# A third, half-width set of k-tiles in the seven-product input projection of an attention layer

## The chip, the cores and the metric

One core of a Trainium2 chip runs one program. The metric is device microseconds (us) of that program, the median of several runs, beside one execution taken by the hardware profiler. Engines: TensorE (PE, with its weight loads PEld), VectorE (DVE), ScalarE (ACT), GpSimd (POOL), SyncE (SP) and 16 DMA engines.

## The reference

Two layers on 256 tokens of width 2048, in fp32: a Mamba2 mixer, then a forgetting-attention mixer, each added to the input, and a last norm. The attention is what the change touches:

```python
h = rmsnorm(x, w)                                  # 256 x 2048
proj = h @ w_in                                    # 2048 x (4 * 4096 + 32): q, k, v, z, forget
log_f = log_sigmoid(f_logit + b_forget); cum = cumsum(log_f)
logits = q @ k.T * scale + cum[query] - cum[key]   # 32 heads of 128, causal
o = softmax(logits) @ v * silu(z)
x = x + o @ w_out
```

## The kernel before

Each fp32 product is made of three in a faster format: a weight tile `raw` is split into a high part `wh` (ACT, `act_hi`, L104) and a low part `wl` (DVE, `dve_lo`, L110), activations likewise, and TensorE adds high x high, high x low and low x high in one PSUM bank (`product`, L130). A weight tile is 128 x 1024: two k-tiles (128 rows of the weight) by 512 columns. Every tile is loaded once, by SP's queue, into one of seven buffers called `raw`; there are five `wh` and four `wl` buffers.

The attention's input projection is done in 16 blocks: for each of eight groups of four heads, a block of q and k and a block of v and z (`block_units`). A block has two token tiles of 128 and two column halves, L and R, of 512. The first `KS` = 8 of the 16 k-tiles are done by seven products of sums in place of eight (a fast matrix product over pairs of k-tiles by pairs of token tiles by column halves): two sets of four k-tiles each. A step such as `A1` makes one of the seven weight sums and multiplies it by one of seven activation sums, the "forms", which are built once (`x2_tiles`, `form_x`, `split_form`) and held in the pool `forms` of six buffers. Weight sums are three chains: "a" is loaded (A0), a term is added by an accumulating DMA of POOL's queue (A1), the sum "b" by DVE (A3, L181), another term by POOL (A2); "b" is loaded (B0) and added to (B1); "c" is loaded (C0). The other eight k-tiles are done plainly, in parts of 12 matmuls, "L" and "R", of two k-tiles each. A step on one set has six matmuls.

`STEPS` writes out the order of a block's steps by hand; `FIRST` is that of the first block, which also holds the forget gate's product and the switch to the attention's pool of buffers. `run` splits the tile of the part three ahead (`AHEAD`) before a part's matmuls, so that ACT and DVE run ahead of TensorE as far as `wh`, `wl` and `raw` buffers are free. Other work is hung on these parts by due times (`later`, `emit_due`, counted in half parts); the instructions of an engine run in program order.

Between the blocks lies the attention of four heads (`four_heads`). For each pair of heads, `load_cum` fetches the cumulated forget logs, broadcast to all partitions (`cB`); `logits` adds them, the query's own sums `cum_q` and the causal mask in two DVE instructions per head (L1142) to a tile `dd`, which `softmax` adds to the scores. After groups 1 to 5 comes one output stage of eight parts (`out_f`), and three follow at the end. So a steady cycle is one q/k block, one v/z block and one output stage.

Of the kernel before, what the change touches and what calls it, by code (L numbers as in the profile page):

```python
# [11 lines left out]
F32 = mybir.dt.float32  # L12
# [5 lines left out]
P = 128  # L18
# [16 lines left out]
C_S = {64: C_MN + 384, 32: C_MN + 384 + 64}  # L35
# [10 lines left out]
KS = 8  # L46
# [3 lines left out]
def constants():  # L50
    c = np.zeros((P, C_N), np.float32)
    i = np.arange(P)
    j, t = i[:, None], i[None, :]
    c[:, C_ID:C_ID + P] = np.eye(P)
    c[:, C_CC:C_CC + P] = ((j >= 64) & (j <= t)) * 1.0 - ((j < 64) & (j > t)) * 1.0
    c[:, C_U:C_U + P] = j > t
    tri = (j <= t) * 1.0
    c[:, C_MQ:C_MQ + 384] = np.concatenate([tri, np.ones((P, P)), tri], 1) * 0.25
    low = np.where(t <= j, 0.0, NEG)
    c[:, C_MN:C_MN + 384] = np.concatenate([low, np.zeros((P, P)), low], 1)  # L60
# [7 lines left out]
def hybrid_kernel(ctx: ExitStack, tc: tile.TileContext, a):  # L68
# [69 lines left out]
    def prep(u, h, pieces=1, first=False):  # L138

        raw = wp.tile([P, 1024], F32, tag="raw", name="raw", bufs=RAW)
        wh = wp.tile([P, 1024], F32R, tag="wh", name="wh")
        m, n = u.get("both", (1024, 0))
        wl = wp.tile([P, 1024], F32R, tag="wl", name="wl", bufs=4) if 2 * n < m else None
        wide = 1024 // m * (m - n)
        for i in range(pieces):
            c = slice(i * wide // pieces, (i + 1) * wide // pieces)
            k = slice(i * 1024 // m // pieces, (i + 1) * 1024 // m // pieces)
            nc.sync.dma_start(raw[:, c], u["src"][:, h * wide + c.start:h * wide + c.stop])  # L150
            if not n:
                act_hi(wh[:, c], raw[:, c])
                dve_lo(wl[:, c], raw[:, c], wh[:, c])
                continue
            r = raw[:, c].rearrange("p (k m) -> p k m", m=m - n)
            hi = wh.rearrange("p (k m) -> p k m", m=m)[:, k]
            if first and i == 0:
                nc.vector.tensor_copy(hi[:, :, :m - n], r)
            else:
                act_hi(hi[:, :, :m - n], r)  # L160
            dve_lo(hi[:, :, m - n:], r[:, :, m - 2 * n:], hi[:, :, m - 2 * n:m - n])
            if wl is not None:
                lo = wl.rearrange("p (k m) -> p k m", m=m)[:, k]
                dve_lo(lo[:, :, :m - 2 * n], r[:, :, :m - 2 * n], hi[:, :, :m - 2 * n])
            if i + 1 < pieces:
                yield
        u["w"][h] = (wh, wl)

    def prep_sum(u):


        name, src, how = u["chain"]
        if how == "load":
            u["sums"][name] = (
                fp[0].tile([P, 1024], F32, tag="sum", name=f"sum_{name}") if u.get("apart") else
                wp.tile([P, 1024], F32, tag="raw", name=f"sum_{name}", bufs=RAW))
            nc.sync.dma_start(u["sums"][name], src)
        elif how == "add":
            behind["POOL"] = nc.gpsimd.dma_start(u["sums"][name], src, accum_op=ALU.add).ins  # L179
# [3 lines left out]
        wh = wp.tile([P, 1024], F32R, tag="wh", name="wh")  # L183
        wl = wp.tile([P, 1024], F32R, tag="wl", name="wl", bufs=4)
        act_hi(wh, raw)
        behind["DVE"] = dve_lo(wl, raw, wh).ins
        u["w"][0] = (wh, wl)
        yield
# [74 lines left out]
    def split_form(f, summed, held, g, name):  # L263
# [8 lines left out]
        gh, gl = (gp.tile([P, 7, P], F32R, tag=f"g{i}", name=f"g{i}{name}") for i in "hl")  # L272
# [30 lines left out]
    def joined(out, ps, scale):  # L303

        n = out.shape[0]
        rest = sp.tile([P, S], F32, tag="rest", name="rest")[:n, :]
# [39 lines left out]
    def ktile(x, k):  # L346

        return x[k // 4][:, k % 4]
# [4 lines left out]
    def row_scale(rst, name, pool=cp):  # L353
# [51 lines left out]
    def xt_split(tag):  # L405
        return [bp.tile([P, 4, 2, S], F32R, tag=f"x{q}", name=f"x{tag}_{q}") for q in range(4)]
# [474 lines left out]
    def x2_tiles(k0):  # L881
# [29 lines left out]
    def stats2():  # L911
# [10 lines left out]
        lay2["rstB"] = row_scale(r, "rstB2")  # L922


    cum_q = cp.tile([P, T2, FH], F32, name="cum_q")
# [18 lines left out]
    def forget_sums(lf):  # L944
# [7 lines left out]
        pq = bank(psa, "pq")  # L952
        nc.tensor.matmul(pq[:, 0:FH], tri, lf[:, 0, :], start=True, stop=True)
# [20 lines left out]
    STEPS = (A0, C0, "L", B0, "L", "L", A1, "L", A3, "R", "R", "R", B1, A2, "R")  # L974
    FIRST = (0, "L", "L", 1, "L", A0, C0, B0, "L", "enter", A1, A3, "R", "R", "R", B1, A2, "R")

    def block_units(w_s, w_p, out, scale, done, order):
# [3 lines left out]
        ps, held, sums = {}, {}, ({}, {})  # L981
        us = {c: [{"src": w_p[i][m], "w": [None, None]} for m in range((KT - KS) // 4)]
              for i, c in enumerate("LR")}

# [19 lines left out]
        def mm_sum(u, form, name, p2):  # L1004
            wh, wl = u["w"][0]
            first = start(name)
            for i, w in enumerate((wh, wh, wl)):
                for p in range(2):
                    y = lay2["forms"][0][2 * p2 + p][i % 2]
                    product(ps[name], y[:, form, :], w[:, p * 512:p * 512 + 512],  # L1010
                            start=first and i == p == 0, stop=p2 == p == 1 and i == 2,
                            skip_group_check=True)

        def mm_rest(u, n, names):
            wh, wl = u["w"][n % 2]
            first = [start(name) for name in names]
            for i, w in enumerate((wh, wh, wl)):
                for k2 in range(2):
                    k = KS + 2 * n + k2
                    for t, name in enumerate(names):  # L1020
# [3 lines left out]
                                stop=2 * n + k2 == KT - KS - 1 and i == 2 and name != "y",  # L1024
# [17 lines left out]
        for step in order[0]:  # L1042
# [6 lines left out]
            if step in n_rest:  # L1049
# [10 lines left out]
            for p2 in range(2):  # L1060
                u = {"chain": (chain, w_s[p2, term], how), "sums": sums[p2], "w": [None],
                     "apart": chain == "b" and p2 == 0 and order[0] is STEPS}
                parts.append({"u": u, "h": [0], "long": 1,
                              "mm": lambda u=u, form=form, name=name, p2=p2:
                                  mm_sum(u, form, name, p2)})
            if (chain, term) in reads:
                parts[-1]["post"] = reads[chain, term]
        if "enter" in order[0]:
# [3 lines left out]
    def four_heads(hq, first=()):  # L1072
# [7 lines left out]
        def vz_done(c):  # L1080
# [3 lines left out]
            vh = fp[0].tile([P, 512], F32R, tag="vh", name=f"vh{hq}")  # L1084
            vl = fp[0].tile([P, 512], F32R, tag="vl", name=f"vl{hq}")
# [19 lines left out]
        def load_cum(i2):  # L1105
            cb = fp[0].tile([P, 2, S], F32, tag="cB", name=f"cB{hq}_{i2}", bufs=2)
            h = 4 * hq + 2 * i2
            with tc.issue_after(behind["POOL"]):
                nc.gpsimd.dma_start(cb, cum_d[h:h + 2, :].partition_broadcast(P))
            st[f"c{i2}"] = cb  # L1110
# [19 lines left out]
        def logits(i):  # L1130
# [5 lines left out]
            h = 4 * hq + i  # L1136
            st["dd"] = dd = fp[0].tile([P, 384], F32, tag="dd", name="dd")
            cb = st[f"c{i // 2}"][:, i % 2, :]
            mk = cst[:, C_MN:C_MN + 384]
            with tc.issue_after(st["split"]):  # L1140
                for t, c, n in BLOCKS:
                    nc.vector.scalar_tensor_tensor(  # L1142
                        dd[:, c:c + n], cb[:, :n], cum_q[:, t, h:h + 1], mk[:, c:c + n],
                        op0=ALU.add, op1=ALU.add)
# [54 lines left out]
        def close(i):  # L1199
# [15 lines left out]
        return [block_units(a["wf_s"][hq, n], a["wf_p"][hq, n], out, scale, done,  # L1215
# [90 lines left out]
def packed(x, norm_w, m_w_in, m_conv_w, m_conv_b, m_dt_bias, m_A_log, m_D,  # L1306
# [46 lines left out]
    def by_k(w):  # L1355
# [13 lines left out]
        "wf_s": np.stack([qk[0], vz[0]], 1), "wf_p": np.stack([qk[1], vz[1]], 1),  # L1369
# [19 lines left out]
```

## Time and profile before

| what | before |
|---|---|
| median of 3 runs | 1591.97 us (1591.59 to 1593.38) |
| the profiled execution's own time | 1592.1 us |
| its span, first to last instruction | 1590.3 us |
| granted TensorE clock | 0.999 |
| HBM read | 357.29 MB, 226 GB/s over the span |
| instructions | 22604 |

How to read it: the span is the time from the first to the last instruction. Busy time is a sum over one engine's instructions; matmuls are pipelined and their ends are modelled, so a TensorE that is always busy need not be at its peak. The chain of waits is followed back from the last instruction to what released it. Rows of transfers give their size and the median time from issue to landing. In a timeline an idle time in brackets stands with what ended it.

### The profile page before, as it was taken

How to read it: one execution, taken by the hardware profiler on the slowest of the kernel's cores; microseconds unless marked ns; L12 is line 12 of the kernel's file. 1: busy time of each engine (PE TensorE's matmuls, PEld its weight loads, DVE VectorE, ACT ScalarE, POOL GpSimd, SP SyncE). 2: the span in 40 equal slices, each digit the busy share in tenths (PEclk: the TensorE clock that was granted, in tenths of full speed). 3: DMA queues.
4: the chain of work that ended last, by engine and by line, in shares of the span. 5: the costliest groups of instructions: out<-in, count | busy, mean ns of one | idle time of the engine just before them, and what ended most of it. 6: DMA issues, size and time to landing. Idle time of an engine off the chain costs nothing.

```text
span 1590.3 us, 22604 instructions
## 1 busy us (share of the span) xinstructions
PE 1576.8 (99%) x7808; PEld 1326.1 (83%) x7808; DVE 1332.9 (84%) x2016; ACT 1058.3 (67%) x1624; POOL 164.7 (10%) x211
## 2 busy tenths in 40 slices
PE   9999999999999999999999999999999999999997
PEld 7888888888888888878888888888888888888886
DVE  6898989798989898788887887878878887888886
ACT  7677676767676765766776675666666666666764
POOL 0000111011100110011110110110110111011100
PEclk9999999999999999999999999999999999999999
DMA  9665798769886987579887887797886887898842
GB/s 369 193 214 189 192 270 221 265 175 273 222 262 182 269 216 236 187 172 251 265 235 252 223 213 247 223 247 213 222 261 187 251 253 182 237 263 242 260 164 80
DMA packets 100356, 360.98 MB, mean 227 GB/s; under 512 B 11505, under 2 KB 12401, under 8 KB 100113
## 3 DMA queue, kind: packets, MB, share of 16 engines
q1 hardware_dynamic: 75312, 270.16, 48.4%
q0 software_dynamic: 24784, 89.24, 29.6%
q8 instruction: 61, 1.00, 0.2%
q14 instruction: 55, 0.44, 0.1%
q10 hardware_dynamic: 144, 0.13, 0.0%
HBM read 357.29 MB, written 2.20 MB: 226 GB/s over the span
## 4 chain that ended last, share of the span: by engine, by line
PE 97%; DVE 1%; issue 0%; DMA 0%; ACT 0%; SPq 0%; ACTq 0%; POOLq 0%; POOL 0%
PE psa L130 24%; PE pst L130 17%; PE psx L130 12%; PE psz L130 10%; PE psv L130 9%; PE psu L130 8%; PE psy L130 8%; PE py L682 2%; PE pqk L1117 1%; PE psc L1135 1%; PE ppt L1171 1%; PE po L1197 0%; PE pof L687 0%; PE psc L1133 0%; PE pyt L737 0%; PE pxa L632 0%
## 5 line engine op out<-in xcount | busy, mean ns | idle before, releaser
L104 ACT ACTIVATE wh<-raw 128x1024 fp32r<-128x1024 f32 (+2 forms) x371 | 390.3, 1054 | 210.1 <-PE psa L130 62.5
L110 DVE TENSOR_TENSOR wl<-raw,wh 128x1024 fp32r<-128x1024 f32 (+2 forms) x371 | 447.2, 1211 | 61.5 <-issue 29.2
L104 ACT ACTIVATE wh<-sum_a 128x1024 fp32r<-128x1024 f32 x176 | 185.4, 1056 | 130.6 <-PE psy L130 29.2
L110 DVE TENSOR_TENSOR wl<-sum_a,wh 128x1024 fp32r<-128x1024 f32 x176 | 214.7, 1222 | 61.2 <-PE psu L130 40.4
L130 PE MATMUL pst<-x,wh 128*128 128x512 f32 (+1 forms) x800 | 203.2, 394 | 2.1 <-ACT wh L104 1.3
L130 PEld LDWEIGHTS pst<-x,wh 128*128 128x128 f32 (+1 forms) x800 | 144.6, 187 | 31.9 <-ACT wh L104 1.9
L130 PE MATMUL psa<-wh,x 128*128 128x512 f32 x512 | 129.5, 392 | 0.0
L104 ACT ACTIVATE wh<-sum_b 128x1024 fp32r<-128x1024 f32 x88 | 93.3, 1060 | 51.9 <-PE psx L130 29.9
L110 DVE TENSOR_TENSOR wl<-sum_b,wh 128x1024 fp32r<-128x1024 f32 x88 | 106.5, 1219 | 10.5 <-issue 9.4
L130 PEld LDWEIGHTS pst<-x,wl 128*128 128x128 f32 x768 | 105.8, 190 | 9.0 <-DVE wl L110 0.9
L130 PEld LDWEIGHTS psa<-wh,x 128*128 128x128 f32 x512 | 95.3, 188 | 20.5 <-DVE cu L308 0.6
L130 PE MATMUL pst<-x,wl 128*128 128x256 f32 x768 | 109.1, 282 | 0.0
L179 POOL DMA_DIRECT2D sum_a<-in_wf_s x64 | 56.1, 878 | 470.0 <-DVE wl L110 311.7
L130 PE MATMUL psz<-wh,x 128*128 128x512 f32 x256 | 100.4, 392 | 0.0
L130 PE MATMUL psv<-wh,x 128*128 128x512 f32 x256 | 99.8, 390 | 0.0
L130 PE MATMUL psu<-wh,x 128*128 128x512 f32 x256 | 99.8, 390 | 0.0
L130 PE MATMUL psy<-wh,x 128*128 128x512 f32 x256 | 99.7, 389 | 0.0
L775 DVE TENSOR_TENSOR xs<-psa,xs 128x512 f32<-128x512 f32 (+1 forms) x81 | 52.0, 679 | 31.7 <-PE psa L130 31.6
L130 PE MATMUL psa<-wh,ghf 128*128 128x512 f32 (+1 forms) x260 | 71.0, 392 | 0.0
L130 PE MATMUL psa<-wl,x 128*128 128x512 f32 x256 | 69.3, 391 | 1.1 <-DVE wl L110 1.0
L130 PE MATMUL psa<-wh,glf 128*128 128x512 f32 (+1 forms) x260 | 69.6, 386 | 0.0
L130 PE MATMUL psa<-wl,ghf 128*128 128x512 f32 (+1 forms) x260 | 69.6, 386 | 0.0
(360 smaller groups left out, 3250.4 us busy)
## 6 DMA issues: line engine op xcount, KB each, us to landing
raw<-in_wf_p SPq DMA_DIRECT2D x128, 512.0 KB, 5.0
raw<-in_wm_t SPq DMA_DIRECT2D x90, 512.0 KB, 5.4
raw<-in_wm_z SPq DMA_DIRECT2D x64, 512.0 KB, 5.7
sum_a<-in_wf_s POOLq DMA_DIRECT2D x64, 512.0 KB, 8.3
raw<-in_wf_o SPq DMA_DIRECT2D x64, 512.0 KB, 5.5
sum_a<-in_wm_s POOLq DMA_DIRECT2D x36, 512.0 KB, 7.4
sum_a<-in_wf_s SPq DMA_DIRECT2D x32, 512.0 KB, 7.6
sum_c<-in_wf_s SPq DMA_DIRECT2D x32, 512.0 KB, 5.9
```

Source lines behind the costliest of these rows:

```text
L104: nc.scalar.activation(out, in_, AF.Copy)
L110: return nc.vector.tensor_tensor(out, in_, hi.bitcast(F32), op=ALU.subtract)
L130: behind["PE"] = nc.tensor.matmul(*args, **kw).ins
L179: behind["POOL"] = nc.gpsimd.dma_start(u["sums"][name], src, accum_op=ALU.add).ins
L682: nc.tensor.matmul(st["py"][t][:, c], m[:, j, t, :], st["xd"][:, t, c], start=True, stop=True)
L775: nc.vector.tensor_tensor(c, pss[t][:, a:b], c, op=ALU.add)
L1117: nc.tensor.transpose(pt[:, n * P:n * P + P], st["qk"][:, t, c:c + FD], ident)
L1135: nc.tensor.matmul(ps[:, P:P + S], q[:, :P], k[:, P:], start=j == 0, stop=j == 2)
L1171: nc.tensor.transpose(pt[:, c:c + P], uu[:, c:c + P], ident)
```

## The change

- `KS` becomes 10 in all blocks but the first: k-tiles 8 and 9 form a third set, half as wide (one pair of k-tiles, weight tiles of 128 x 512). Its steps have three matmuls. The first block keeps 8 k-tiles, with its own weights `wf_b`. L and R have three parts each in place of four, and the order of the steps is new: A2 is last.
- The third set's sums lie in the sixth buffer of the pool `forms` ("a" with tag `gh`, "b" with tag `gl`); its "c" takes a `raw` buffer. A fifth form is built; its unsplit values take a `raw` buffer for that time.
- The query's own sums are left out (`cum_q` and its three products): they are the same for a whole row of the softmax. The cumulated logs are loaded straight into `dd`, now two buffers for two heads each, and the mask is added to two heads by one DVE instruction.
- Buffers move to make room: the activations' k-tiles are cut 4, 4, 2, 2, 4, and `vh`, `vl` take the place of k-tiles 8 and 9; `rest`, `cu`, `vt` and the row of scales move to the Mamba pool; split outputs of groups 0 to 5 move from `forms` to the attention's pool.

```diff
-KS = 8
+KS = 10
+KS0 = 8
+X_AT = (0, 4, 8, 10, 12)
...
         name, src, how = u["chain"]
+        wide = u.get("wide", 1024)
         if how == "load":
-            u["sums"][name] = (
-                fp[0].tile([P, 1024], F32, tag="sum", name=f"sum_{name}") if u.get("apart") else
-                wp.tile([P, 1024], F32, tag="raw", name=f"sum_{name}", bufs=RAW))
+            if u.get("apart"):
+                t = fp[0].tile([P, 1024], F32, tag="sum", name=f"sum_{name}")
+            elif wide < 1024 and name != "c":
+                t = gp.tile([P, 7, P], F32, tag="gh" if name == "a" else "gl",
+                            name=f"sum_{name}").rearrange("p m s -> p (m s)")
+            else:
+                t = wp.tile([P, 1024], F32, tag="raw", name=f"sum_{name}", bufs=RAW)
+            u["sums"][name] = t[:, :wide]
...
-        gh, gl = (gp.tile([P, 7, P], F32R, tag=f"g{i}", name=f"g{i}{name}") for i in "hl")
+        if pool is None:
+            gh, gl = (gp.tile([P, 7, P], F32R, tag=f"g{i}", name=f"g{i}{name}") for i in "hl")
+        else:
+            gh, gl = (pool.tile([P, 4, P], F32R, tag=f"f{i}", name=f"g{i}{name}", bufs=2)
+                      for i in "hl")
...
-            f = lp.tile([P, 4 * (S + 1)], F32, tag=("xa", "xa", "xd", "zs")[k0 // 2],
-                        name="form", bufs=2 if k0 < 4 else 1)
+            f = (lp.tile([P, 4 * (S + 1)], F32, tag=("xa", "xa", "xd", "zs")[k0 // 2],
+                         name="form", bufs=2 if k0 < 4 else 1) if k0 < 8 else
+                 wp.tile([P, 1024], F32, tag="raw", name="form", bufs=RAW))
...
-        pq = bank(psa, "pq")
-        nc.tensor.matmul(pq[:, 0:FH], tri, lf[:, 0, :], start=True, stop=True)
-        nc.tensor.matmul(pq[:, FH:2 * FH], ones, lf[:, 0, :], start=True, stop=False)
-        nc.tensor.matmul(pq[:, FH:2 * FH], tri, lf[:, 1, :], start=False, stop=True)
-        nc.scalar.copy(cum_q.rearrange("p t h -> p (t h)"), pq[:, :2 * FH])
...
-    STEPS = (A0, C0, "L", B0, "L", "L", A1, "L", A3, "R", "R", "R", B1, A2, "R")
+    STEPS = (A0, C0, "L", B0, "L", A1, "L", A3, "R", "R", B1, "R", A2)
...
         def right():
             add("z", 0, 1, ALU.subtract)
             add("u", 1, 1, ALU.subtract, 0)
+
+        def last():
             add("y", 1, 0)
             done(held["out"])
...
-            for p2 in range(2):
-                u = {"chain": (chain, w_s[p2, term], how), "sums": sums[p2], "w": [None],
+            for p2 in range(len(pairs)):
+                u = {"chain": (chain, w_s[p2][term], how), "sums": sums[p2], "w": [None],
+                     "wide": 512 * pairs[p2],
                      "apart": chain == "b" and p2 == 0 and order[0] is STEPS}
-                parts.append({"u": u, "h": [0], "long": 1,
+                steps[0] += pairs[p2] == 1
+                parts.append({"u": u, "h": [0], "long": 1 if pairs[p2] == 2 else steps[0] % 2,
...
-            with tc.issue_after(st["split"]):
-                for t, c, n in BLOCKS:
-                    nc.vector.scalar_tensor_tensor(
-                        dd[:, c:c + n], cb[:, :n], cum_q[:, t, h:h + 1], mk[:, c:c + n],
-                        op0=ALU.add, op1=ALU.add)
+            if i % 2 == 0:
+                dd = st[f"d{i // 2}"].rearrange("p h (b s) -> p h b s", b=3)
+                mk = cst[:, C_MN:C_MN + P].unsqueeze(1).unsqueeze(1).to_broadcast([P, 2, 2, P])
+                with tc.issue_after(st["split"]):
+                    nc.vector.tensor_tensor(dd[:, :, 0:3:2], dd[:, :, 1:3], mk, op=ALU.add)
...
+        def weights(n):
+            s1, s2 = a["wf_s"][hq, n], a["wf_h"][hq, n]
+            half = lambda c, m: a["wf_p"][hq, n, c][:, m * 1024:m * 1024 + 1024]
+            rest = [[half(c, m) for m in range((KT - KS) // 2)] for c in range(2)]
+            if hq == n == 0:
+                return [s1[0], s1[1]], [[a["wf_b"][c], *rest[c]] for c in range(2)]
+            return [s1[0], s1[1], s2], rest
```

More of the change, by code (lines that the diff above doesn't have):

```diff
@@ L59, in constants @@
     low = np.where(t <= j, 0.0, NEG)
-    c[:, C_MN:C_MN + 384] = np.concatenate([low, np.zeros((P, P)), low], 1)
+    c[:, C_MN:C_MN + P] = low
     for n, at in C_S.items():
@@ L149, in prep @@
             k = slice(i * 1024 // m // pieces, (i + 1) * 1024 // m // pieces)
-            nc.sync.dma_start(raw[:, c], u["src"][:, h * wide + c.start:h * wide + c.stop])
+            src = u["halves"][h] if "halves" in u else u["src"][:, h * wide:(h + 1) * wide]
+            nc.sync.dma_start(raw[:, c], src[:, c])
             if not n:
@@ L182, in prep_sum @@
         raw = u["sums"][name]
-        wh = wp.tile([P, 1024], F32R, tag="wh", name="wh")
-        wl = wp.tile([P, 1024], F32R, tag="wl", name="wl", bufs=4)
+        wh = wp.tile([P, 1024], F32R, tag="wh", name="wh")[:, :wide]
+        wl = wp.tile([P, 1024], F32R, tag="wl", name="wl", bufs=4)[:, :wide]
         act_hi(wh, raw)
@@ L305, in joined @@
         n = out.shape[0]
-        rest = sp.tile([P, S], F32, tag="rest", name="rest")[:n, :]
+        rest = lp.tile([P, S], F32, tag="rest", name="rest", bufs=2)[:n, :]
         nc.scalar.copy(rest, ps[:n, S:])
@@ L346, in ktile, with row_scale @@
     def ktile(x, k):
-        return x[k // 4][:, k % 4]
+        q = max(i for i in range(5) if X_AT[i] <= k)
+        return x[q][:, k - X_AT[q]]
     def token(x, k, t):
         return [ktile(x, k)[:, i, t * P:t * P + P] for i in range(2)]
-    def row_scale(rst, name, pool=cp):
+    def row_scale(rst, name, pool):
         ps = bank(psa, "psr")
@@ L405, in xt_split @@
     def xt_split(tag):
-        return [bp.tile([P, 4, 2, S], F32R, tag=f"x{q}", name=f"x{tag}_{q}") for q in range(4)]
+        return [bp.tile([P, n, 2, S], F32R, tag=f"x{q}", name=f"x{tag}_{q}")
+                for q, n in enumerate((4, 4, 2, 2, 4))]
     x1 = xt_split(1)
@@ L921, in stats2 @@
         nc.vector.tensor_scalar(rq, r, FD ** -0.25, None, op0=ALU.mult)
-        lay2["rstB"] = row_scale(r, "rstB2")
-    cum_q = cp.tile([P, T2, FH], F32, name="cum_q")
+        lay2["rstB"] = row_scale(r, "rstB2", lp)
     cum_d = dram.tile([FH, S], F32, name="cum_d")
@@ L973, in hybrid_kernel @@
     B0, B1, C0 = ("b", 3, "load", 3, "z"), ("b", 1, "add", 6, "x"), ("c", 2, "load", 1, "v")
-    STEPS = (A0, C0, "L", B0, "L", "L", A1, "L", A3, "R", "R", "R", B1, A2, "R")
+    STEPS = (A0, C0, "L", B0, "L", A1, "L", A3, "R", "R", B1, "R", A2)
     FIRST = (0, "L", "L", 1, "L", A0, C0, B0, "L", "enter", A1, A3, "R", "R", "R", B1, A2, "R")
     def block_units(w_s, w_p, out, scale, done, order):
-        ps, held, sums = {}, {}, ({}, {})
-        us = {c: [{"src": w_p[i][m], "w": [None, None]} for m in range((KT - KS) // 4)]
+        ps, held, sums = {}, {}, ({}, {}, {})
+        us = {c: {"src": None, "halves": w_p[i], "w": [None] * len(w_p[i])}
               for i, c in enumerate("LR")}
+        pairs = (2, 2, 1)[:len(w_s)]
+        n_l = KT - 2 * len(w_p[0])
+        steps = [0]
         def start(name):
@@ L1007, in mm_sum @@
             for i, w in enumerate((wh, wh, wl)):
-                for p in range(2):
+                for p in range(pairs[p2]):
                     y = lay2["forms"][0][2 * p2 + p][i % 2]
                     product(ps[name], y[:, form, :], w[:, p * 512:p * 512 + 512],
-                            start=first and i == p == 0, stop=p2 == p == 1 and i == 2,
+                            start=first and i == p == 0,
+                            stop=i == 2 and (p2, p + 1) == (len(pairs) - 1, pairs[-1]),
                             skip_group_check=True)
         def mm_rest(u, n, names):
-            wh, wl = u["w"][n % 2]
+            wh, wl = u["w"][n]
             first = [start(name) for name in names]
@@ L1067, in block_units @@
                 parts[-1]["post"] = reads[chain, term]
+        if order[0][-1] == A2:
+            parts[-1]["post"] = last
+        else:
+            parts[-1]["post"] = lambda: [right(), last()]
         if "enter" in order[0]:
@@ L1105, in load_cum @@
         def load_cum(i2):
-            cb = fp[0].tile([P, 2, S], F32, tag="cB", name=f"cB{hq}_{i2}", bufs=2)
+            dd = fp[0].tile([P, 2, 384], F32, tag="dd", name=f"dd{hq}_{i2}", bufs=2)
             h = 4 * hq + 2 * i2
             with tc.issue_after(behind["POOL"]):
-                nc.gpsimd.dma_start(cb, cum_d[h:h + 2, :].partition_broadcast(P))
-            st[f"c{i2}"] = cb
+                nc.gpsimd.dma_start(dd[:, :, P:], cum_d[h:h + 2, :].partition_broadcast(P))
+            st[f"d{i2}"] = dd
         def turn_qk(i):
@@ L1207, in close @@
             if i % 2:
-                split = lambda form=st["form"]: split_form(form, False, gated2, hq,
-                                                           f"f{hq}_{i // 2}")
+                split = lambda form=st["form"]: split_form(
+                    form, False, gated2, hq, f"f{hq}_{i // 2}", fp[0] if hq < G - 2 else None)
                 if hq == G - 2:
@@ L1213, in close @@
                     later(1, split)
-        return [block_units(a["wf_s"][hq, n], a["wf_p"][hq, n], out, scale, done,
+        def weights(n):
[5 more added lines that the diff above has]
+            return [s1[0], s1[1], s2], rest
+        return [block_units(*weights(n), out, scale, done,
                             (FIRST, first) if hq == n == 0 else (STEPS, ()))
```

44 lines of the change are left out of this document (22 added, 22 removed).

## The prediction

> **What bounds the kernel now.** I read the page's busy times first, then the chain that ended last, then stages.
>
> ```profile
> PE 1576.8 (99%) x7808; PEld 1326.1 (83%) x7808; DVE 1332.9 (84%) x2016; ACT 1058.3 (67%) x1624; POOL 164.7 (10%) x211
> q1 hardware_dynamic: 75312, 270.16, 48.4%
> q0 software_dynamic: 24784, 89.24, 29.6%
> PE 97%; DVE 1%; issue 0%; DMA 0%; ACT 0%; SPq 0%; ACTq 0%; POOLq 0%; POOL 0%
> ```
>
> The chain is 97% TensorE. I then look at the spacing of matmuls in the chain, and at one steady cycle (two blocks of the attention's inputs and one output stage).
>
> ```profile
> 1089.27 13.61 PE psa L130 x60
> 1313.78 13.61 PE psa L130 x60
> 977.00:1089.30 112.30, 112.30 (x534) 93.97 (x533) 91.21 (x124) 72.50 (x105) 11.65 (x14) 1.00 0.81 230
> ```
>
> Sixty 512-column matmuls take 13.61 us: 226.8 ns each, alike in stages 224 us apart, at clock 1.00. The window's columns are length, busy us of PE, PEld, DVE, ACT, POOL, clock, DMA share, GB/s: PE never pauses, DVE has 21 us left of 112.3, DMA 19%. So TensorE is the bound, with DVE and DMA next.
>
> A busy PE row could also hold slack between matmuls; the even 226.8 ns says that it does not, so every matmul taken out counts in full.
>
> **The change, part by part.**
>
> *Matmuls.* Two k-tiles done plainly are 2 x 2 token tiles x 2 column halves x 3 = 24 matmuls; as seven products of sums they are 7 x 3 = 21. Three fewer in each of 15 blocks (all but the first): 45 x 226.8 ns = 10.2 us off the path. The row term's running sums go too.
>
> ```profile
> 723.07 0.41 PE L953 MATMUL pq<-lf,cst 128*128 128x32 f32 x2
> 723.76 0.71 PE L130 MATMUL psx<-wh,ghx 128*128 128x512 f32 x2
> ```
>
> L953 to L955 occupy PE from 723.07 to 723.76: 0.7 us more. Together -10.9 us.
>
> *DVE, ACT and POOL.* Per cycle, four plain 1024-wide tiles go, 14 half-width sum tiles and two half-width adds come; eight three-input adds at L1142 become two 512-wide ones.
>
> ```profile
> L110 DVE TENSOR_TENSOR wl<-raw,wh 128x1024 fp32r<-128x1024 f32 x25 | 30.2, 1220 | 1.9 <-issue 1.6
> L104 ACT ACTIVATE wh<-raw 128x1024 fp32r<-128x1024 f32 x24 | 25.4, 1060 | 14.7 <-PE psu L130 5.5 <-PE psa L130 3.3 <-PE psz L130 1.5
> L110 DVE TENSOR_TENSOR glf<-form,ghf 128x512 fp32r<-128x512 f32 x2 | 1.4, 690 | 0.1
> L104 ACT ACTIVATE ghf<-form 128x512 fp32r<-128x512 f32 x2 | 1.2, 624 | 1.2 <-DVE form L1203 1.2
> L1142 DVE SCALAR_TENSOR_TENSOR dd<-cB,cum_q,cst 128x256 f32<-128x256 f32 x4 | 1.9, 479 | 0.0
> L1142 DVE SCALAR_TENSOR_TENSOR dd<-cB,cum_q,cst 128x128 f32<-128x128 f32 x4 | 1.4, 345 | 0.0
> L179 POOL DMA_DIRECT2D sum_a<-in_wf_s x8 | 7.0, 880 | 64.5 <-DVE wl L110 64.5
> ```
>
> DVE: 14 x 0.69 + 2 x 0.69 - 4 x 1.22 - 4 x (0.479 + 0.345) + 2 x 0.69 = +4.2 us (the 512-wide row stands for all new 512-wide adds), so 95.4 of a cycle of 112.3 - 6 x 0.2268 = 110.9 us, 86%. ACT: 14 x 0.624 - 4 x 1.06 = +4.5, so 77 us, 69%. POOL issues six more accumulating transfers, 5.3 us, so 17 us; they queue behind one another ahead of the cum_d loads, which are needed later. I cost these at nothing: the cover is DVE's 21 us.
>
> *Transfers.* The page's queue rows give 0.484 x 1590.3 / 270.16 = 2.85 us of all 16 DMA engines per MB for plain loads, and 0.296 x 1590.3 / 89.24 = 5.27 for POOL's, nearly all accumulating. Per block, plain loads change by three halves for two full tiles (-0.26 MB, -0.7 us), accumulating ones by three halves (+0.79 MB, +4.1 us): +3.4 us per block. Bounds: +1.5 if an accumulating half costs no more than a plain one (0.79 x 2.85 - 0.75), +9.8 if a 256 KB transfer held the engines as long as a 512 KB one (1 x 0.524 x 2.85 + 3 x 0.524 x 5.27). Near which end?
>
> ```profile
> out<-xs SPq DMA_DIRECT2D x4, 256.0 KB, 2.4
> out<-xs SPq DMA_DIRECT2D x2, 512.0 KB, 3.2
> raw<-in_wf_f SPq DMA_DIRECT2D x1, 256.0 KB, 2.6
> sum_a<-in_wf_s SPq DMA_DIRECT2D x32, 512.0 KB, 7.6
> sum_b<-in_wf_s SPq DMA_DIRECT2D x32, 512.0 KB, 4.5
> sum_a<-in_wf_s POOLq DMA_DIRECT2D x64, 512.0 KB, 8.3
> ```
>
> Halving the output's transfer saves 0.8 us, as much as 0.26 MB at 2.85 us per MB (0.75): bytes, so +3.4. Against the stages:
>
> ```profile
> 688.00:723.80 35.80, 35.80 (x161) 28.50 (x160) 31.61 (x45) 23.21 (x27) 5.20 (x6) 1.00 0.81 230
> 723.80:764.70 40.90, 40.90 (x183) 33.87 (x183) 31.76 (x31) 24.30 (x27) 7.01 (x9) 1.00 0.94 269
> 878.00:923.20 45.20, 45.20 (x220) 38.01 (x219) 37.06 (x52) 30.86 (x48) 5.21 (x6) 1.00 0.81 223
> 923.20:967.60 44.40, 44.40 (x210) 36.98 (x209) 35.72 (x44) 29.35 (x41) 4.62 (x6) 1.00 0.87 253
> 967.60:990.50 22.90, 22.90 (x107) 19.01 (x106) 18.31 (x29) 12.20 (x19) 1.82 (x2) 1.00 0.68 193
> ```
>
> These are the first block, the second, a steady q/k block, its v/z block, and an output stage. A steady v/z block asks DMA for 0.87 x 44.4 + 3.4 = 42.0 of 43.7 us (96%), a q/k block for 40.0 of 44.5; the output stage's 32% idle restores the lead. The second block asks 0.94 x 40.9 + 3.4 = 41.8 of 40.2 us: short by 1.6. Bounds there: 0 if loads run ahead, 4.3 if DMA cannot exceed its 0.94. I take 1.6, the balance itself.
>
> *Entry of the attention.* A fifth form is built for k-tiles 8 and 9, and it holds one of seven raw tiles while it is built.
>
> ```profile
> 682.40 1.09 DVE L110 TENSOR_TENSOR glx<-form,ghx 128x896 fp32r<-128x896 f32 x1
> 683.41 0.89 DVE L271 TENSOR_TENSOR form<-form 128x128 f32<-128x128 f32 x4
> 717.53 1.22 DVE L110 TENSOR_TENSOR wl<-sum_a,wh 128x1024 fp32r<-128x1024 f32 x1
> 719.01 0.63 PE L130 MATMUL psy<-wl,ghx 128*128 128x512 f32 x2
> ```
>
> It adds 1.09 + 0.89 = 2.0 us to DVE where DVE is busy in 31.6 of 35.8 us; at the block's end the low part of A2 is ready at 718.75 and PE takes it at 719.01, a lead of 0.26 us. Bounds: 0, if the wait for other things absorbs it, and 3.5, if the missing raw tile delays a load by another 1.5 (one tile, 0.524 x 2.85). I take 1.5, near the 2.0 - 0.26 that the lead cannot cover.
>
> *Waits that move.* The half-width sum "a" lives in the one sixth buffer that the five held forms leave. So the next block's half load of A0 cannot start before this block's half of A2 is split. In the steps' new order A2 comes last, so only two full steps lie between. Queued behind it on SP are loads of C0 and L.
>
> ```profile
> 1124.60 0.87 POOL L179 DMA_DIRECT2D sum_a<-in_wf_s  x1 [0.49 <-DVE wl L110]
> 1135.23 1.06 ACT L104 ACTIVATE wh<-sum_a 128x1024 fp32r<-128x1024 f32 x1 [1.71 <-DMA sum_a<-in_wf_s]
> 1136.99 0.40 PE L130 MATMUL psz<-wh,x 128*128 128x512 f32 x1
> 1139.93 1.23 DVE L110 TENSOR_TENSOR wl<-sum_a,wh 128x1024 fp32r<-128x1024 f32 x1 [0.81 <-PE psu L130]
> 1143.81 0.62 PE L130 MATMUL psy<-wh,ghx 128*128 128x512 f32 x2
> ```
>
> Today A2's second tile lands at 1135.2, 10.6 us after its issue, and PE needs it at 1143.8; its low part waits only for a free wl buffer. With four wl buffers A2's half can be split when the last R part starts: call that 0. It is done by 1.2 (0.62 + 0.69, partly overlapped). PE needs A0's half after R (12 matmuls), A2 (15) and two full A0 steps (12): 39 x 0.2268 = 8.8. The load must land by 8.8 - 0.6 (ACT) = 8.2, so it has 7.0 us. Rows: 2.6 for an idle 256 KB load, 4.5 and 7.6 for crowded 512 KB ones. At 4.5 nothing is lost; at 7.6 0.6 us, at each of nine block changes with no output stage between (5.4 us). I take 4.5, because A2's transfer is then over, but 1.0 us in all for the two early changes where the lead is thin; bounds 0 and 5.4.
>
> The Trainium skill's page "DMA: Bandwidth & Descriptors" (section Anatomy of one DMA — SWDGE (gpsimd) path) puts a transfer at about 2.0 us plus its bytes at 436 GB/s, 2.6 us for a load of this size. The idle row agrees, the crowded ones do not; by the page the 1.0 us would be 0 and the sum 1.0 us lower.
>
> Buffers moved without work (vh and vl, rest, cu, split forms) cost nothing: each is released a cycle, or over 20 us, before its next use; what covers them is the same lead.
>
> **Sum.** The profiled execution took 1592.1 us (span 1590.3, the rest lies around it; the median of the runs is 1591.97, 0.1 lower). 1592.1 - 10.9 + 1.5 + 1.6 + 1.0 = 1585.3; I say 1585. All costs at their low ends: 1581.2. All at their high ends: 1592.1 - 10.9 + 3.5 + 4.3 + 5.4 = 1594.4.
>
> **Rivals.**
>
> (a) *DMA becomes the bound in the v/z blocks* (slower). For: 42.0 us of 43.7, and accumulating transfers can start only when the previous sum is split, so DMA idles in spots; the busiest block so far reached 0.94. Against: that block still kept PE full. If a v/z block reaches a share s, it lasts 42.0 / s. At 0.90 this is 46.7, or 3.0 us lost in each of eight: -10.9 + 4.1 + 24 = 1609; at 0.93 1.5 us each, 12 in all, 1597. It decides from 42.0 / (43.7 + 0.9) = 0.94 downward, where 8 x 0.9 eats the 6.8 us left. The same comes about if halves hold the engines not by bytes but as their landing times stand, 2.4 to 3.2 or 75% of a full one: +0.25 x 1.49 + 2.25 x 2.76 = 6.6 us per block (1.49 and 2.76 are a full tile's, 0.524 MB at the two prices), 45.2 in a v/z block, 1.5 lost in eight, 1597; I give this 0.03 of the 0.13.
>
> By the same page of the Trainium skill (same section) the fixed 2.0 us would make a half 81% of a full one if it were time of the engines, and the sum about 1603 us, an estimate from that page. The 0.8 us between the two output rows speaks against it.
>
> (b) *The single buffer of the half sum stalls every change*, as at 7.6 us or 1 us more because C0's loads go ahead of it: 0.6 to 1.2 us at nine places, 1590 to 1595. For: landing times of 7.6 in the crowded stage. Against: the lead counted above.
>
> (c) *Matmul time saved, DVE too late at the row of nine sum steps* A2, A0, C0: PE 45 x 0.2268 = 10.2 us, DVE 6 x 1.22 + 3 x 0.69 = 9.4 plus three PSUM adds. If each crossing cost 0.5 us more, 1589 to 1591, no change. Against: DVE enters it several parts ahead.
>
> **How the numbers follow.** Measurements of this kernel tell 0.2% (3.2 us) from no change. Forecast (1581 to 1588.8): 0.67. Rival (a): 0.13, mostly slower. (b): 0.12, half no change and half slower or on the edge. (c): 0.08, no change mostly. Faster 0.67, same 0.17, slower 0.16. The likeliest case's own range is 1581 to 1589; the range, to leave out no more than the outer parts of (a), is 1580.5 to 1596.
>
> **What would show it.** PE's matmul count falls by 45 and 6 to about 7757; the steady cycle shrinks from 112.3 to about 110.9 us with PE still filling the window, DVE near 95 and DMA share near 0.87. Between 688 and 765 us PE gains nothing net. Wrong, if in steady cycles ACT waits on DMA of sum_a and PE's idle time stands behind it (a, b), or behind DVE wl (c).

## The result and the profile after

The changed kernel takes 1633.76 us (median of 4 runs, 1629.87 to 1635.13), the kernel before 1592.12 beside it: ratio 1.0257, 95% interval 1.0244 to 1.0270. It is slower by 41.6 us where 6.8 us less was forecast. The profiled execution took 1629.87 us, span 1627.9, granted clock 0.991. Ratios and intervals here and below come from fast runs; the only slow one, 3206.9 us, is one of the ten of "A3 ahead of the third L" and moves that median by 0.1 us.

The page's busy times, its queue rows and the chain's shares:

```profile
PE 1585.0 (97%) x7757; PEld 1324.7 (81%) x7757; DVE 1356.6 (83%) x2063; ACT 1074.8 (66%) x1701; POOL 205.8 (13%) x256
q1 hardware_dynamic: 77472, 266.10, 46.4%
q0 software_dynamic: 31264, 101.04, 32.8%
PE 77%; DMA 10%; issue 7%; DVE 3%; POOL 2%; ACT 1%; POOLq 0%; ACTq 0%; DVEq 0%; SPq 0%
```

The 51 matmuls are gone (7808 to 7757). But PE now stands idle for 1627.9 - 1585.0 = 42.9 us, against 1590.3 - 1576.8 = 13.5 before: 29.4 us more. And its busy time is not 10.9 us less but 8.2 more, so what remains runs 19.1 us slower. 29.4 + 19.1 - 10.9 = 37.6, the difference of the spans. The chain, 97% PE before, holds 10% of DMA. Which transfer it is, the chain in order of time says (start, length, what), with two marks one steady cycle apart:

```profile
917.77 12.10 DMA sum_b<-in_wf_h
1000.43 10.89 PE psa L132 x48
1034.51 11.66 DMA sum_b<-in_wf_h
1115.34 10.89 PE psa L132 x48
```

It is nearly always the same one, with 8 of the 10%: B1's half-width accumulating load. The rows of the transfers (count, KB each, median us from issue to landing) and of the waits (us in all, times, longest) name its size and its victim:

```profile
sum_b<-in_wf_s POOLq DMA_DIRECT2D x32, 512.0 KB, 5.5
sum_b<-in_wf_h POOLq DMA_DIRECT2D x15, 256.0 KB, 11.7
ACT wh L106 <- DMA sum_b<-in_wf_h: 80.3, 14, 9.2
```

Half the bytes take twice as long. The timelines of POOL, ACT and PE in one steady block show why:

```profile
914.00 0.85 POOL L188 DMA_DIRECT2D sum_b<-in_wf_s  x1 [1.87 <-DVE sum_a L190]
916.03 0.85 POOL L188 DMA_DIRECT2D sum_a<-in_wf_s  x1 [1.18 <-DVE wl L112]
917.17 0.85 POOL L188 DMA_DIRECT2D sum_a<-in_wf_s  x1 [0.29 <-DVE wl L112]
917.77 1.14 POOL L188 DMA_DIRECT2D sum_b<-in_wf_h  x1
922.85 0.51 ACT L106 ACTIVATE qkh<-pqk 128x384 fp32r<-128x384 f32 x1
930.25 0.63 ACT L106 ACTIVATE wh<-sum_b 128x512 fp32r<-128x512 f32 x1 [6.90 <-DMA sum_b<-in_wf_h]
930.79 0.25 ACT L1204 COPY p<-ppt 128x128 f32<-128x128 f32 x1
931.09 0.73 PE L1217 MATMUL po<-p,vz 128*128 128x128 f32 x2 [2.22 <-ACT p L1204]
```

POOL issues B1's third load not behind B1's first two, but behind both full loads of A2, which PE needs later. POOL's issues go out in the order of its instructions in the program. A2's loads wait for `wl` of A3's first two tiles, B1's half for DVE's addition for A3's half, which comes after them on DVE; presumably that is why the scheduler, which orders the instructions when the program is built, put A2's first; no run shows its reason. So the half lands at 929.9, ACT waits 6.90 us for it, and the attention's copy of p, behind it on ACT, holds PE for 2.22 us. In 8 of the 15 blocks the half stands behind two of A2's full loads, in 5 behind one, in 2 behind none.

The rest of the cycle is as forecast (length; busy us of PE, PEld, DVE, ACT, POOL; clock, DMA share, GB/s):

```profile
1000.43:1115.34 114.91, 112.07 (x527) 92.85 (x527) 94.23 (x131) 74.18 (x115) 17.12 (x20) 1.00 0.86 234
```

DVE 94.2 (95.4 forecast), ACT 74.2 (77), POOL 17.1 (17), DMA 0.86; only the length is 114.9 and not 110.9.

### The profile page after: what moved, and what is told of

Its sections match the earlier page's. It is cut to its first block, busy times and chain, and to the rows that moved or that the text cites. A ratio compares the mean times of both kernels' runs of the same rounds, so it can differ in the third digit from the quotient of the medians.

```text
span 1627.9 us, 22941 instructions
## 1 busy us (share of the span) xinstructions
PE 1585.0 (97%) x7757; PEld 1324.7 (81%) x7757; DVE 1356.6 (83%) x2063; ACT 1074.8 (66%) x1701; POOL 205.8 (13%) x256
## 3 DMA queue, kind: packets, MB, share of 16 engines
q0 software_dynamic: 31264, 101.04, 32.8%
## 4 chain that ended last, share of the span: by engine, by line
PE 77%; DMA 10%; issue 7%; DVE 3%; POOL 2%; ACT 1%; POOLq 0%; ACTq 0%; DVEq 0%; SPq 0%
PE psa L132 21%; PE pst L132 16%; PE psx L132 10%; DMA sum_b<-in_wf_h 8%; PE psz L132 7%; PE psv L132 6%; PE psy L132 5%; PE psu L132 3%; PE py L697 2%; DVE wl L112 1%; DMA sum_a<-in_wf_s 1%; POOL sum_a L188 1%; DMA raw<-in_wf_p 1%; ACT wh L106 1%; PE pqk L1141 1%
## 5 line engine op out<-in xcount | busy, mean ns | idle before, releaser
L112 DVE TENSOR_TENSOR wl<-raw,wh 128x1024 fp32r<-128x1024 f32 (+2 forms) x341 | 410.1, 1211 | 69.0 <-issue 24.4
L106 ACT ACTIVATE wh<-raw 128x1024 fp32r<-128x1024 f32 (+2 forms) x341 | 355.5, 1051 | 139.4 <-PE psa L132 52.0
L106 ACT ACTIVATE wh<-sum_a 128x1024 fp32r<-128x1024 f32 (+1 forms) x236 | 220.4, 946 | 124.0 <-PE psa L132 31.1
L112 DVE TENSOR_TENSOR wl<-sum_a,wh 128x1024 fp32r<-128x1024 f32 (+1 forms) x236 | 251.7, 1084 | 29.4 <-ACT wh L106 22.2
L106 ACT ACTIVATE wh<-sum_b 128x1024 fp32r<-128x1024 f32 (+1 forms) x118 | 110.1, 951 | 112.5 <-DMA sum_b<-in_wf_h 80.3
L112 DVE TENSOR_TENSOR wl<-sum_b,wh 128x1024 fp32r<-128x1024 f32 (+1 forms) x118 | 126.2, 1085 | 63.0 <-ACT wh L106 62.1
L132 PEld LDWEIGHTS psa<-wh,x 128*128 128x128 f32 x512 | 95.4, 188 | 20.2 <-issue 0.5
L132 PE MATMUL psx<-wh,ghx 128*128 128x512 f32 x237 | 81.5, 410 | 10.4 <-ACT wh L106 10.2
L132 PE MATMUL psx<-wh,glx 128*128 128x512 f32 x237 | 79.5, 401 | 0.0
L132 PE MATMUL psx<-wl,ghx 128*128 128x512 f32 x237 | 78.6, 398 | 0.1
L106 ACT ACTIVATE wh<-sum_c 128x1024 fp32r<-128x1024 f32 (+1 forms) x59 | 53.9, 942 | 27.6 <-PE psa L132 17.4
```

The lines of the kernel that those rows point to most:

```text
L106: nc.scalar.activation(out, in_, AF.Copy)
L112: return nc.vector.tensor_tensor(out, in_, hi.bitcast(F32), op=ALU.subtract)
L132: behind["PE"] = nc.tensor.matmul(*args, **kw).ins
```

## The experiments

Theory Q: the place of B1's half on POOL's queue. Theory D, the forecast's rival (a): the accumulating transfers ask more of DMA than there is. Theory S, its rival (b): the single buffer of the half sum "a".

**POOL in the order of the steps.**

```diff
-            behind["POOL"] = nc.gpsimd.dma_start(u["sums"][name], src, accum_op=ALU.add).ins
+            with tc.issue_after(behind["POOL"]) if "POOL" in behind else ExitStack():
+                behind["POOL"] = nc.gpsimd.dma_start(u["sums"][name], src, accum_op=ALU.add).ins
```

> The changed kernel, with POOL's accumulating loads issued in the order of the steps, so that the half-width load of B1 goes ahead of the two full ones of A2. Theory Q (the order on POOL's queue): B1's half then lands some 4 to 6 us after its issue rather than 11.7 (256 KB behind at most its own two full loads), ACT's 80.3 us of waiting on it fall below 25 and most of the 4.0 us that a steady cycle has over its 110.9 come back: 1597 to 1608 us. Theory D (the accumulating transfers take more of DMA than there is): the same bytes must still move, so 1625 to 1633. Theory S (the single buffer of the half sum a): no change either, 1625 to 1633.

Measured: 1600.92 us, ratio 1.0052 (1.0036 to 1.0068): 32.8 of the 41.6 us are back. The timelines of POOL and ACT in the same block, and the row of the transfer:

```profile
908.44 0.85 POOL L189 DMA_DIRECT2D sum_b<-in_wf_s  x1 [1.87 <-DVE sum_a L191]
912.45 0.85 POOL L189 DMA_DIRECT2D sum_b<-in_wf_h  x1 [3.16 <-issue]
912.98 2.08 POOL L189 DMA_DIRECT2D sum_a<-in_wf_s  x2
918.21 0.63 ACT L106 ACTIVATE wh<-sum_b 128x512 fp32r<-128x512 f32 x1 [0.43 <-DMA sum_b<-in_wf_h]
sum_b<-in_wf_h POOLq DMA_DIRECT2D x15, 256.0 KB, 5.8
```

The same transfers, the same bytes; the half lands 5.8 us after its issue, no longer 11.7. ACT waits 0.43 us here, and 4.0 us for it in the whole kernel, no longer 80.3. Q holds; D and S, which expected no change, do not explain the bulk. The Trainium skill's page "DMA: Bandwidth & Descriptors" (section Two DMAs through the same engine are not ordered) says that within one queue of one DMA engine descriptors start in order but are pipelined; the two landing times agree with it.

**The third R ahead of B1**, alone and with the order on POOL (B1's post then also does what `right` did).

```diff
-    STEPS = (A0, C0, "L", B0, "L", A1, "L", A3, "R", "R", B1, "R", A2)
+    STEPS = (A0, C0, "L", B0, "L", A1, "L", A3, "R", "R", "R", B1, A2)
```

> The changed kernel, with the third R part moved ahead of B1 (R R R B1 A2 in place of R R B1 R A2): B1's half gets one R part, 12 matmuls or 2.72 us, more after A3; POOL's order stays. Theory Q: each block's stall behind B1's half (2.4 us in steady blocks, 4 to 6 in two v/z blocks) shrinks by up to 2.72 us, 1600 to 1612. Theory D: no change, 1625 to 1633. Theory S: A2's half comes 2.72 us nearer to the next block's half load of A0, so slower: 1632 to 1650.

> Both edits of the two runs before together. Theory Q: nothing of B1's half is late any more; what is left is the first block's 5.5 us and whatever is late next: 1586 to 1598. Theory D: 1620 to 1633. Theory S: 1630 to 1650, by A0's half load.

Measured: alone 1614.51 us, 1.0133 (1.0115 to 1.0151); with the order 1596.41, 1.0028 (1.0016 to 1.0039). Alone it gives back 19 us, just outside Q's range, because the half still stands behind loads of A2 in 13 blocks and lands late (11.7 us); after the order it is worth 4.5 us more, inside Q's range. S's expected loss did not come.

**The third set's loads on POOL's queue made plain.**

```diff
-            behind["POOL"] = nc.gpsimd.dma_start(u["sums"][name], src, accum_op=ALU.add).ins
+            how = {} if wide < 1024 else {"accum_op": ALU.add}
+            behind["POOL"] = nc.gpsimd.dma_start(u["sums"][name], src, **how).ins
```

> The changed kernel, with the third set's loads on POOL's queue made plain: the three half-width additions of a block are left out of the transfer (the tile is overwritten), while queue, place in it, bytes and waits stay. Theory D: each block's accumulating halves cost 0.79 MB x (5.27 - 2.85) = 1.9 us of all engines less, more than half of the 3.4 us added, so at least half of the 48.7 us between 1629.9 and 1592.1 - 10.9 comes back: below 1608. Theory Q: B1's half is still behind two full accumulating loads and lands only its own 0.6 us earlier: 1618 to 1629.

Measured: 1611.61 us, 1.0120 (1.0101 to 1.0140). Neither range holds it: 22 us back, where Q allowed 16 and D asked for 26, so this run does not decide between them. The half now lands 10.5 us after its issue, 1.2 earlier and not 0.6. ACT's wait for it falls from 80.3 to 56.0 us, more than 1.2 us in each of the 13 blocks where it stands behind A2; why more, stays open.

**Own sums alone**, on the kernel before: its six matmuls (L953 to L955) out, `dd` in two tiles for two heads as in the change, `KS` still 8.

> The kernel before, with only the row's own running sums left out and the two heads' masked sums built in place in one tile (the change's other half; the products of sums stay at eight k-tiles). By the prediction's step: -0.7 us, 1591.0 to 1592.3. Rival: the load of cum_d now waits on POOL's queue until the softmax of two heads earlier has let go of its tile (18.7 us over 4 waits in the changed kernel), and the accumulating loads behind it come late: 1595 to 1605.

Measured: 1591.20 us, 0.9995 (0.9986 to 1.0003), 7802 matmuls. The rival's waits are there, by the profile's waits of POOL:

```profile
POOL dd L1102 <- PE ppt L1160: 27.6, 4, 6.9
```

But they cost no time that can be measured: alone, this half of the change is innocent.

**The entry.** With order and steps mended, most of what is left in the profile lies at 700 to 760 us, where the attention begins. First the fifth form in the forms' sixth buffer in place of a raw tile; then, besides, its split moved later; then, besides, the row term's sums on PE moved later.

```diff
-                 wp.tile([P, 1024], F32, tag="raw", name="form", bufs=RAW))
+                 gp.tile([P, 7, P], F32, tag="gh", name="form").rearrange("p m s -> p (m s)"))
-                    later(2 + q, lambda q=q: form_x(q))
+                    later(2 + q if q < 4 else 15, lambda q=q: form_x(q))
-            later(5, lambda: forget_sums(lf))
+            later(7, lambda: forget_sums(lf))
```

> The run with order and steps (1596.4 us, 1.0028), with the fifth form built in the sixth buffer of the forms in place of a raw tile. Theory R (the missing raw tile delays loads at the entry): ACT's wait of 2.67 us on A2's second load at 719.5 goes, the log chain behind it on ACT and the two gaps of 1.8 and 2.4 us shrink: 1591 to 1594. Theory V (DVE's and ACT's 2.0 and 0.94 us of work on the form are in the way of A1 and A3): no change, 1595.3 to 1597.5.

> The run with order and steps, with the fifth form in the forms' sixth buffer and, besides, its split moved behind A1 and A3, to where DVE stood idle for 2.7 us twice at 714 and 718 us. Theory V: the gap of 1.9 us at 703 goes, and the rest of the block follows earlier: 1590 to 1593. Theory R alone: as the run with the buffer alone, within 1 us. Rival: the split stretches the chain of the logarithms that PE waits for at 726.6 us, and gives the gain back: 1594 to 1598.

> The run with the late form split (1591.4 us), with TensorE's sums for the row term issued two full parts later (seven in place of five after the logarithms), so that PE doesn't wait 3.07 us at 722.3 for lf. If that gap is a wait alone: 1588 to 1589. Rival: cum_d comes later, POOL's loads of it and the first heads' scores with it, and PE waits there instead: 1590.5 to 1592.

Measured: 1593.93 us, 1.0008 (0.9999 to 1.0017); 1591.38, 0.9996 (0.9987 to 1.0005); 1589.44, 0.9983 (0.9974 to 0.9992). The 60 us of the entry, as a window of the changed kernel:

```profile
700.00:760.00 60.00, 54.53 (x230) 43.40 (x229) 50.15 (x62) 33.69 (x39) 12.60 (x15) 0.97 0.87 227
```

The same window of the last of the three:

```profile
700.00:760.00 60.00, 60.00 (x264) 48.81 (x263) 51.90 (x69) 36.93 (x45) 12.28 (x15) 1.00 0.97 255
```

5.5 us of idle PE and a clock of 0.97 have become a full window; order and steps had little part in it, for with these two alone PE is busy for 54.36 us of it at a clock of 0.97. How the idle time came about, in the changed kernel's timelines of ACT and PE:

```profile
719.07 1.06 ACT L106 ACTIVATE wh<-sum_a 128x1024 fp32r<-128x1024 f32 x1 [2.33 <-DMA sum_a<-in_wf_s]
720.04 0.24 ACT L385 ACTIVATE ls_e<-ls_e 128x64 f32<-128x64 f32 x1
728.75 0.62 PE L962 MATMUL pk<-cst,lf 128*32 128x256 f32 x2 [2.21 <-DVE lf L954]
```

The same two instructions with the split moved:

```profile
713.32 0.24 ACT L386 ACTIVATE ls_e<-ls_e 128x64 f32<-128x64 f32 x1
725.62 0.62 PE L963 MATMUL pk<-cst,lf 128*32 128x256 f32 x2 [2.90 <-DVE lf L955]
```

And the matmul with the row sums moved, too:

```profile
725.49 0.62 PE L963 MATMUL pk<-cst,lf 128*32 128x256 f32 x2
```

In the changed kernel the logarithm's step on ACT stands behind the split of A2's second tile, which waits for its transfer until 719.07, so DVE's chain to lf is late and PE, which reaches lf's matmuls in order, waits. Moving the split brought the step to 713.3, but PE was there earlier too and waited 2.90; only the later place of the row sums removed the wait. The step on ACT is not the whole of it, as lf on DVE shows, first in the kernel before, then with the split moved:

```profile
721.21 0.22 DVE L938 SCALAR_TENSOR_TENSOR lf<-vf,ls_q 128x64 f32<-128x64 f32 x1
725.35 0.22 DVE L955 SCALAR_TENSOR_TENSOR lf<-vf,ls_q 128x64 f32<-128x64 f32 x1
```

The step on ACT comes at 713 us in both. But between the steps of the logarithm DVE now does seven splits, the form's own among them, where the kernel before has four.

By their medians the three are worth 2.5, 2.5 and 1.9 us, 7.0 together. The buffer alone lies in theory R's range, but not by R's way: ACT still waits 2.65 us for A2's second load and the logarithm's step comes at 719.8; what shrank is PE's wait at 705 us, from 1.72 to 0.56. The split moved lies in theory V's range, the row sums between their two forecasts. Neighbouring intervals overlap, and a loss of clock of 1.7 us (last section) falls into some executions and not into others; only the sum of the three is clear of that.

**A3 ahead of the third L**, with the order on POOL: three full parts between A3 and B1 as before, and nine sum steps in a row, not twelve.

```diff
-    STEPS = (A0, C0, "L", B0, "L", A1, "L", A3, "R", "R", B1, "R", A2)
+    STEPS = (A0, C0, "L", B0, "L", A1, A3, "L", "R", "R", B1, "R", A2)
```

> POOL in the order of the steps, and the steps A0 C0 L B0 L A1 A3 L R R B1 R A2: three full parts between A3 and B1, as in the kernel before, but R still between B1 and A2, so that nine sum steps stand in a row and not twelve. If the 0.7 us that each v/z block still loses at its start come from the row of twelve: 1592 to 1595.5. Rival: A3 right behind A1 waits for DVE's add and two splits of A1, about 1 us in each of 15 blocks: 1605 to 1615.

Measured: 1597.01 us, 1.0028 (1.0018 to 1.0037), outside both ranges. The steady cycle, though, is what the forecast said:

```profile
986.73:1097.62 110.89, 110.89 (x527) 92.80 (x527) 94.39 (x131) 74.45 (x115) 17.20 (x20) 1.00 0.88 243
```

PE full, 110.89 us, with DMA at 0.88. By its profile, the entry, which this run leaves as it was, and the edges between some blocks keep the time up; the last three runs show such an edge.

**All edits together**; that with the third set's loads made plain; and that with POOL's order left to the scheduler.

> All edits that helped, together: POOL in the order of the steps; steps with A3 ahead of the third L (cycle 110.9 us); the fifth form in the forms' buffer, split late; the row term's sums two parts later. By theory Q and the entry's parts, idle time of PE above that of the kernel before should be 3 to 4 us in all: 1592.1 - 10.9 + 3.6 = 1585, 1583.5 to 1587. Theory D: no version with these bytes gets below the kernel before by more than 0.2%: 1589 or more.

> The version with all edits, with the third set's loads on POOL's queue made plain (the half-width additions are left out; the tile is overwritten). Theory Q: with the order right the cost of these transfers is covered, so no change against the version with all edits, within 1.5 us. Theory D: the 1.9 us of all engines that each block saves come back at least in the v/z blocks, 5 us or more faster.

> The version with all edits but the forced order on POOL: B1's half then stands behind one of A2's two full accumulating loads in 11 of 15 blocks (in the changed kernel: behind two in 8 and one in 5). Theory Q, with 1.5 to 2.5 us of PE idle for each full load that stands ahead where the steps give three full parts: some of it covered, 1588 to 1600. Theory that the three parts between A3 and B1 are what counts and POOL's order does not: as the version with all edits, within 1 us.

Measured: 1590.91 us, 0.9993 (0.9985 to 1.0002); 1586.43, 0.9957 (0.9944 to 0.9971); 1594.27, 1.0016 (1.0006 to 1.0026). The last one separates order from lead: all else alike, the free order costs some 3.4 us (the intervals are apart), and the half's landing time goes with its place: 5.1 us behind no load of A2, 8.2 with one ahead in 11 of 15 blocks, 11.7 in the changed kernel.

The version with all edits misses my 1583.5 to 1587 and lies where theory D put it, at 1589 or more. Timelines of DVE, ACT and PE at the end of its second block, with two transfers from its chain of waits (start, length):

```profile
758.31 0.69 DVE L112 TENSOR_TENSOR wl<-sum_a,wh 128x512 fp32r<-128x512 f32 x1 [0.23 <-ACT wh L106]
759.03 7.30 DMA sum_a<-in_wf_h
1408.55 7.04 DMA sum_a<-in_wf_h
766.43 0.63 ACT L106 ACTIVATE wh<-sum_a 128x512 fp32r<-128x512 f32 x1 [4.39 <-DMA sum_a<-in_wf_h]
767.11 0.50 PE L132 MATMUL psx<-wh,ghx 128*128 128x512 f32 x1 [0.39 <-ACT wh L106]
769.64 0.74 PE L132 MATMUL psv<-wl,ghx 128*128 128x512 f32 x2 [0.38 <-DVE wl L112]
773.04 0.50 PE L132 MATMUL psv<-wl,ghx 128*128 128x512 f32 x1 [0.80 <-DVE wl L112]
```

That is theory S after all, in small: the next block's half load of A0 can start only when DVE has split this block's half of A2, at 759.0, and takes 7.3 us, more than the 7.0 that the forecast left it. ACT and DVE split C0's tiles behind it, and PE waits 1.6 us in three pieces; before, PE had no such wait. The same comes again at 1416 us, behind the load of 7.04 us, with 2.3 us.

Plain loads take off some 4.5 us, between Q's 1.5 and D's 5. In the profiled executions 3.5 us show, half of them idle time of PE, and not at every edge: at the second block's end A0's half takes 7.4 us and PE waits 2.5 us. At the later edge it is issued at 1407.60 and ACT has it at 1413.00:

```profile
1407.60 0.33 SPq L186 DMA_DIRECT2D sum_a<-in_wf_h  x1
1413.00 0.63 ACT L106 ACTIVATE wh<-sum_a 128x512 fp32r<-128x512 f32 x1 [2.16 <-DMA sum_a<-in_wf_h]
```

There PE does not wait. The steady cycle gains nothing. The version with all edits:

```profile
979.02:1089.91 110.89, 110.89 (x528) 92.82 (x527) 94.19 (x130) 74.59 (x115) 17.20 (x20) 1.00 0.87 242
```

The same with plain loads:

```profile
980.76:1091.65 110.89, 110.89 (x527) 92.79 (x527) 94.17 (x130) 74.79 (x115) 15.26 (x20) 1.00 0.84 242
```

0.87 or 0.84 of DMA, the cycle is 110.89. So D's capacity is not the bound in the steady state; a transfer's own time counts where a load has a short lead. For the kernel as a whole D's limit is not refuted: the median of every version that does all the additions stays above 1589 us.

## Why the prediction was wrong

*The bound and the matmuls* were right: 7757 matmuls, and a cycle of 110.89 us, to the tenth, once nothing else stood in the way.

*DVE, ACT and POOL* is the step that failed, in its words on POOL's six new issues: "they queue behind one another ahead of the cum_d loads, which are needed later. I cost these at nothing: the cover is DVE's 21 us." The sizes were right (94.2, 74.2 and 17.1 us). But a sum of busy times is no cover for a transfer's place on a queue. The forecast asked what POOL's six extra issues delay behind them, the cum_d loads, and not what stands ahead of each new issue: two 512 KB accumulating loads that are needed later. The kernel before had the sign: A2's second tile, last of four loads on that queue, took the 10.6 us to land that the forecast itself quotes. Nor did it go on from there to ACT, which waits in order, and to the attention's copies queued behind that wait. Order alone is 32.8 us of the 41.6.

*The new order of the steps* belongs to the same failure. Before, three R parts lay between A3 and B1, now two: 2.72 us less lead for B1's chain of addition, split, load and split. The diff shows it, and the forecast costed the new order only for A2 and A0. With POOL's order mended it is 4.5 us.

*Transfers* were right in bytes and price (0.87 forecast for a cycle; 0.86 to 0.88 measured), so rival (a) did not decide the 41.6 us. The second block's 1.6 us of shortage is not seen up to 760 us: the last entry run keeps PE full from 700 at a DMA share of 0.97, above the 0.94 that I took as the limit. At the block's end PE does wait (1.72 us there, 1.6 with all edits), for A0's half. Plain loads lower the DMA share over 715 to 764 us from 0.99 to 0.93 and leave that wait (2.5 us), which speaks for the single buffer and against a shortage. The changed kernel lost more just behind it, in the third block, and by B1's half again (ACT and PE):

```profile
814.93 0.63 ACT L106 ACTIVATE wh<-sum_b 128x512 fp32r<-128x512 f32 x1 [9.12 <-DMA sum_b<-in_wf_h]
815.61 0.80 PE L132 MATMUL psx<-wh,ghx 128*128 128x512 f32 x1 [3.44 <-ACT wh L106]
```

*Entry, 1.5 us*: mis-sized; it measures 7.0 us. The forecast looked at the lead of A2's low part alone. In the changed kernel PE waits 1.46 us for that, but also 1.72 us at A3 (705 us) and 2.21 us for lf, whose matmuls it takes in order.

*The single buffer, 1.0 us*: right in kind, mis-sized: with all edits 1.6 us of idle PE at the second block's end and 2.3 us at 1416 us, inside its bounds of 0 to 5.4. *Rival (c)*, DVE too late, had no run of its own; in the changed kernel's steady cycle from 1000.43 PE waits 1.65 and 1.00 us for ACT and 0.19 us for DVE. *Own sums, -0.7*: -0.8 by the ratio 0.9995, within its interval.

So successive runs take 32.8 (order), 4.5 (third R), 2.5, 2.5 and 1.9 us (entry) off the 1633.8, by their medians, which leads to 1589.4 us: 2.9 less than the kernel before beside it (0.9974 to 0.9992 of it), at the edge of what a measurement of this kernel can tell. From there to the forecast's 1585.3 some 4 us stay open. Late half loads of A0 hold part of them, and the price of the accumulating transfers may: only the version without the half-width additions comes near, at 1586.4.

## What to carry to other kernels

When a change adds transfers to a queue, list, for one block, what each queue will hold in order, and for each new transfer what stands ahead of it and how long that takes; then follow the engine that waits for it to whatever is queued behind that wait. Free busy time on that engine and free bandwidth say nothing about it. Where the order comes from a scheduler, pin it if two chains with different deadlines share a queue: here one line was worth 33 us.

## What the runs showed of the hardware

Some short stalls were paid twice. In the changed kernel PE stood idle for 2.22 us before 931.09 (the row in the first section), for 1.65 us before 1047.11 and for 2.24 us before 1277.11. Its windows of 4 us behind the three:

```profile
931.00:935.00 4.00, 3.91 (x14) 3.43 (x15) 3.44 (x9) 2.89 (x5) 0.00 (x0) 0.57 0.92 342
1047.11 0.49 PE L1217 MATMUL po<-p,vz 128*128 128x128 f32 x2 [1.65 <-ACT p L1204]
1047.20:1051.20 4.00, 4.00 (x21) 3.45 (x22) 3.44 (x10) 3.33 (x5) 0.00 (x0) 1.00 1.03 363
1277.11 0.49 PE L1217 MATMUL po<-p,vz 128*128 128x128 f32 x2 [2.24 <-ACT p L1204]
1277.11:1281.11 4.00, 4.00 (x21) 3.49 (x22) 3.43 (x10) 3.32 (x4) 0.00 (x0) 1.00 0.95 343
```

A stall of the run with the late row sums, with the window behind it, and the window behind the 2.90 us of the run with the split moved (its row at 725.62 above):

```profile
768.49 0.50 PE L132 MATMUL psx<-wh,ghx 128*128 128x512 f32 x1 [1.72 <-ACT wh L106]
768.50:772.50 4.00, 4.00 (x11) 2.64 (x12) 3.74 (x5) 4.00 (x7) 1.60 (x2) 0.71 1.04 195
725.62:729.62 4.00, 4.00 (x18) 3.05 (x19) 4.00 (x5) 2.52 (x5) 1.42 (x2) 1.00 1.04 197
```

The granted clock, the last column but two, fell to 0.57 and 0.71 after 2.22 and 1.72 us, and stayed at 1.00 after 1.65, 2.24 and 2.90. So the length of a stall alone does not tell whether the clock falls. Where it falls, 0.43 of 4 us is 1.7 us, nearly the stall again. Over the whole execution (0.999 - 0.991) x 1627.9 = 13 us of clock were lost, by the rounded clocks, most of the 19.1 us by which PE's busy time is longer than its matmuls explain. The order on POOL brought it back: at a clock of 0.999 the same 7757 matmuls keep PE busy for 1572.8 us, 12.2 less, and the other 18.4 us of the 30.6 between the two spans are idle time. The Trainium skill's page "TensorE: Matmul & The Clock Gate" (Part 1: The HAM clock gate) has the clock halved after an idle window of about 3.4 us, counted in windows that run freely. That it falls agrees; here idle times of 1.7 and 2.2 us were enough in some places and 2.9 us were not in another, so a stall of that length should be priced at between once and about twice itself.
